# Layer 1's experts for 64 tokens by gathered rows, and GpSimd passes moved

## The chip, the core and the metric

The kernel runs on one core of a Trainium2 chip. Five engines work from queues of their own, in the order in which instructions were put there: TensorE (PE; its weight loads are PEld), VectorE (DVE), ScalarE (ACT), GpSimd (POOL) and SyncE (SP, which issues most DMAs). The metric is the device time of one execution, in microseconds.

## The reference, cut to what matters

Two layers act on 256 context and 256 latent tokens of width 1024. Layer 0 mixes by latent attention and retention, layer 1 by a gated delta net; after each mixer stands a norm and then PEER, a table of 16,384 experts:

```python
q = (xb @ w_q).reshape(PEER_BLOCK, PEER_HEADS, 2, half)
v1, i1 = lax.top_k(s1, PEER_TOPK)          # 16 best of 128 keys, twice
sc, j = lax.top_k(cand, PEER_TOPK)         # 16 best of the 256 sums, per head
gate = jax.nn.softmax(sc.astype(F32), axis=-1)
act = jax.nn.gelu(jnp.einsum('phkd,pd->phk', u_tab[e_idx], xb))
return jnp.einsum('phk,phkd->pd', gate * act, v_tab[e_idx])
```

So a token has 8 heads x 16 = 128 slots, each an expert with a row of 1024 in `u_tab` and one in `v_tab`. Layer 0 does this for all 512 tokens (four blocks of 128), layer 1 for the 256 latent ones (two blocks). Only the latent tokens are returned.

## The kernel before

**Two ways to compute PEER.** The dense way (`Dense`) runs over all 16,384 experts in 128 chunks of 128. Per chunk, `act` multiplies the chunk's u table (stationary, 128x128) by the tokens' columns (moving), 8 slices of depth; ScalarE takes gelu; VectorE multiplies by the tokens' weights for these experts, which `route` has spread into a table W in DRAM; and `products` multiplies the result (stationary, 128 experts x 128 tokens) by the chunk's v table (moving, two halves of 512 columns) into PSUM sums f that stay there over the whole stage. Two chunks form a group. The other way (`Rows`) takes 128 tokens as partitions and gathers for each of the 128 slots one row per token: GpSimd issues the indirect DMA, VectorE reduces u row times token to one value, and adds gate times v row to `rowy`. Before, layer 0 has three dense blocks (384 columns) and one by rows; layer 1 has two dense blocks (256 columns).

**Precision.** Every fp32 operand of the large products is split into a high part, rounded to the one-pass type fp32r, and a low part (`split`): ScalarE copies the high part (ush, vsh, gsh), VectorE or GpSimd subtracts (usl, vsl, gsl), and `mm3` makes three matmuls: high-high, high-low, low-high.

**Stages of one PEER.** `route` first chooses: per query table j a projection (pq), scores (sc), and scans for the 16 best on VectorE; the query tables' splits are GpSimd's (usl at L271), except the first two. Then it decodes gates and expert numbers and spreads them into W, 16 tokens at a time. Beside both, `Dense.early` computes the act values of the first chunks (36 and 24) and puts them to DRAM (gelud). Then `Dense.run` goes through the chunks; `fill` hangs other work on chunk numbers: in layer 0 the reductions for later modulation vectors (ada units, adaj at L341), the rows' steps, and `affine`, the first norm's scale and shift of four token tiles by GpSimd (L425, L426), and in layer 1 `affine` of two tiles at chunk 2.

**Who sets the order.** The loops only say what depends on what, and in which order of preference. The instructions of each engine are put in their order when the program is built, by a scheduler that takes what it holds to be ready; the queues then run in that fixed order. A step that hangs on a late chunk may stand much earlier in a queue.

**The first mixer.** 16 projections (z) and the retention values (rvp) with weight splits by GpSimd (arwl), beside 24 ada units on VectorE. `modulate` (L443 to L447) turns four slices of the normed tokens after another into hp: transposes, scale and shift on VectorE, high part by ScalarE, low part by VectorE and GpSimd in turn.

Of the kernel before, what the change touches and what calls it, by code (L numbers as in the profile page):

```python
# [47 lines left out]
RING = 4, 3  # L48
# [90 lines left out]
def layout(i):  # L139
# [42 lines left out]
    a["p_v"] = np.ascontiguousarray(i["peer_v"].reshape(2, NE, P, D))  # L182
    a["p_ur"] = np.ascontiguousarray(i["peer_u"][0])
# [59 lines left out]
class Model:  # L243
# [186 lines left out]
    def modulate(self, pool, ps, l, m, x, s, hs, i0, ln):  # L430
# [8 lines left out]
        for k in range(KD):  # L439
# [6 lines left out]
            nc.scalar.copy(hs[0][:, k, sl], t)  # L446
            (nc.gpsimd if k % 2 else nc.vector).tensor_sub(hs[1][:, k, sl], t, hs[0][:, k, sl].bitcast(F32))  # L447
# [20 lines left out]
    def mixer0(self, open_x, open_h):  # L468
# [150 lines left out]
        with ExitStack() as e2:  # L619
# [9 lines left out]
            weave(low(), pipe([key()] + [ret_proj(j) for j in range(4, 16)], 2), units())  # L629
            weave(ret_v())  # L630
# [143 lines left out]
        with ExitStack() as e2:  # L774
            p = self.pool(e2, "m0o", 1, side="right")
            w = []
            for k in range(KD):
                r = p.tile([P, D], F32, tag="woutr", name=f"woutr{k}", bufs=3)
                nc.sync.dma_start(r, a["ar_out"][:, k, :])
                w.append(self.split(p, r, [P, D], f"wout{k}", eng=nc.gpsimd if k % 3 == 2 else nc.vector))  # L780
                next(rest, None)
# [31 lines left out]
    def route(self, l, hs, parts, ps, first, dense, e2, rows=None):  # L813
        nc, a, c = self.nc, self.a, self.c
        nb = sum(len(tbs) for tbs in parts)
        spread_tbs = [tb for tbs in parts for tb in tbs if rows is None or tb != rows.tb]
        wd = self.dram.tile([len(spread_tbs) * P // WG, P, NE, WG], F32, name=f"W{l}")
# [13 lines left out]
        nc.sync.dma_start(kT, a["p_k"][l])  # L831

# [56 lines left out]
        def choose(part):  # L889
# [6 lines left out]
            while True:  # L896
                ends = [next(g, pr) is pr for g in (pr, tp)]
                if all(ends):
                    return
                if ends[0]:  # L900
                    n += 1
                    step(1 + n % 2)
                yield
# [63 lines left out]
        def slots(tb):  # L967
            t = f"{l}{tb}"
            g = gates[tb][0]
            tr = ps.tile([P, 512], F32, tag="ps", name="tr" + t)  # L970
            for n in range(2):
                nc.tensor.transpose(tr[:, n * P:(n + 1) * P], place(tb, n), c["ident"])
# [9 lines left out]
        def spread(tb, HA):  # L982
            t = f"{l}{tb}"
            for gi in range(P // OH):
# [29 lines left out]
        for part in range(len(parts)):  # L1014
            weave(choose(part))
        eq_.close()
        dense.by = None
        for part, tbs in enumerate(parts):
# [3 lines left out]
            for i, tb in enumerate(tbs):  # L1022
                if i + 1 < len(tbs):
                    slots(tbs[i + 1])
                elif rows is not None:
# [6 lines left out]

    class Rows:
        def __init__(self, m, tb, pool):
            self.m, self.tb = m, tb
            self.h = pool.tile([P, D], F32, name="rowh")
            self.e = pool.tile([P, P], U32, name="rowe")
            self.g = pool.tile([P, P], F32, name="rowg")
            self.y = pool.tile([P, D], F32, name="rowy")
            self.act = pool.tile([P, P], F32, name="rowa")  # L1040


        def choose(self, g, ii, hs, ps):
            nc, c = self.m.nc, self.m.c
            nc.vector.scalar_tensor_tensor(self.e, ii[0], float(NE), ii[1], ALU.mult, ALU.add)
            nc.vector.tensor_scalar_mul(self.g, g.rearrange("p h k -> p (h k)"), 1.0 / 1024)
            nc.gpsimd.memset(self.y, 0.0)
            ts = slice(self.tb * P, (self.tb + 1) * P)
            for h in range(2):
                o = ps.tile([P, 512], F32, tag="ps", name=f"rowt{h}")  # L1050
                for i in range(4):
                    for z in range(2):
                        self.m.mm(o[:, i * P:(i + 1) * P], hs[z][:, 4 * h + i, ts].bitcast(F32), c["ident"], z == 0, z == 1)
# [3 lines left out]
        def steps(self, pool):  # L1057
            m, nc = self.m, self.m.nc
            tabs = m.a["p_ur"], m.a["p_v"][0].rearrange("n p d -> (n p) d")
            rows = {}  # L1060

            def gather(z, s):
                if 0 <= s < P:
                    t = rows[z, s] = pool.tile([P, D], F32, tag="row" + "uv"[z], name=f"row{'uv'[z]}{s}", bufs=RING[z])
                    nc.gpsimd.indirect_dma_start(t, None, tabs[z], bass.IndirectOffsetOnAxis(ap=self.e[:, s:s + 1], axis=0))  # L1065

            for s in range(RING[0]):
                gather(0, s)
            for s in range(P + LAG):
                if s < P:  # L1070
# [4 lines left out]
                gather(0, s + RING[0])  # L1075
                gather(1, s - LAG + RING[1])
                if s % 4 == 1 and 5 <= s < P + 4:
# [3 lines left out]
                if v >= 0:  # L1081
                    nc.vector.scalar_tensor_tensor(self.y, rows.pop((1, v)), self.g[:, v:v + 1], self.y, ALU.mult, ALU.add)  # L1082
# [3 lines left out]
    class Dense:  # L1086
        G = 2

        def __init__(self, m, l, hs, nb, pool, done):
            self.m, self.l, self.hs, self.nb, self.p, self.done = m, l, hs, nb, pool, done  # L1090
# [3 lines left out]
        def early(self, es, ps):  # L1094
            m, N = self.m, self.nb * P
# [5 lines left out]
        def ahead(self, order, ps):  # L1101
            m, nc, l = self.m, self.m.nc, self.l
            us = self.table(order[0])
            for n, c in enumerate(order):
# [10 lines left out]
                else:  # L1115
                    g = self.pg.tile([P, self.nb * P], F32, tag="gelus", name=f"gelus{l}{c}", bufs=3)
                    nc.scalar.activation(g, o[:, :self.nb * P], AF.Gelu)
# [9 lines left out]
        def product(self, o, us, k):  # L1127
            N = self.nb * P
            self.m.mm3(o[:, :N], (us[0][:, k, :], us[1][:, k, :]), (self.hs[0][:, k, :N], self.hs[1][:, k, :N]), k == 0, k == KD - 1)

        def gelu(self, c, o):
            N = self.nb * P
# [15 lines left out]
        def run(self, wd, pool, psa, psv, fill, sums=None, ready=None):  # L1148
            m, nc, l, nb, G, done = self.m, self.m.nc, self.l, self.nb, self.G, self.done
            N = nb * P  # L1150
# [4 lines left out]
            def fetch(c):  # L1155
                late = c >= NE - 2
                vr = (self.p if late else pool).tile([P, D], F32, tag="ur" if late else "vr", name=f"vr{l}{c}", bufs=2)
                nc.sync.dma_start(vr, m.a["p_v"][l, c])
# [5 lines left out]
            def weighted(c, vr):  # L1164
# [8 lines left out]
                gs = m.split(pool, g, [P, N], "gs", bufs=GBUFS[l])  # L1173
                return gs, vs or m.split(pool, vr, [P, D], "vs", bufs=VBUFS[l])

# [628 lines left out]
```

## Time and profile before

| | |
|---|---|
| median of 3 runs | 3058.61 us (3046.81 to 3059.09) |
| profiled execution | 3056.68 us, span 3054.9 us, mean TensorE clock 0.955 |
| busy share of the span | PE 91%, PEld 79%, DVE 74%, ACT 42%, POOL 21% |
| DMA | 643.85 MB, 211 GB/s over the span |
| layer 0's dense stage | about 727 to 1692 us |
| layer 1's dense stage | about 2375 to 3037 us |

Matmul durations overlap each other, so TensorE's pace is read from starts, from the chain of waits or from counts in a window, and not from a mean duration. A window's row gives for each engine its busy time in the window and, in brackets, its instructions.

### The profile page before, as it was taken

To read this page: it belongs to the slowest core of one execution; us is meant where nothing else is said; L and a number is where in the kernel's file an instruction comes from. 1 tells how busy PE (TensorE), PEld (TensorE's weight loads), DVE (VectorE), ACT (ScalarE), POOL (GpSimd) and SP (SyncE) were. 2 spreads that over 40 slices of the span, in tenths; PEclk is the share of its full clock that TensorE was granted. 3 is DMA by queue.
4 is the path that set the end of the run, shared out by engine and by line. 5 is a ranking of instruction groups with operands and counts; after the bars stand their busy time and mean duration, and the time that the engine had idled before them with its cause. 6 is when DMAs were issued, how large, how long until landed. Compare 5 with 4: busy or idle time off the path is not lost.

```text
span 3054.9 us, 44722 instructions
## 1 busy us (share of the span) xinstructions
PE 2773.7 (91%) x16867; PEld 2412.5 (79%) x16867; DVE 2249.5 (74%) x4414; ACT 1291.4 (42%) x2176; POOL 643.4 (21%) x413
## 2 busy tenths in 40 slices
PE   7988898987999789999999899678878899999997
PEld 4766788986788688888899677667877689999996
DVE  2976599796999898999744578876898655555555
ACT  3335333674333233333333356333457454444443
POOL 2410134001036765666100000122400100000000
PEclk9999899998999999999999899788999999999999
DMA  6531223668999799999744123313348866666763
GB/s 231 186 121 45 95 89 109 232 236 318 325 360 390 284 400 374 394 397 395 250 153 135 57 73 94 91 56 119 117 152 296 262 221 207 215 213 207 214 206 110
DMA packets 272168, 643.85 MB, mean 211 GB/s; under 512 B 36464, under 2 KB 138992, under 8 KB 267472
## 3 DMA queue, kind: packets, MB, share of 16 engines
q1 hardware_dynamic: 225120, 487.50, 47.7%
q0 software_dynamic: 38768, 142.49, 12.0%
q10 hardware_dynamic: 8064, 11.01, 1.0%
q8 instruction: 132, 2.16, 0.3%
q14 instruction: 84, 0.69, 0.1%
HBM read 583.77 MB, written 57.15 MB: 210 GB/s over the span
## 4 chain that ended last, share of the span: by engine, by line
PE 35%; DVE 13%; issue 9%; DMA 8%; POOL 5%; ACT 3%; POOLq 0%; DVEq 0%; ACTq 0%; SPq 0%
PE f L254 14%; PE act L254 13%; DMA rowv<-p_v,rowe 3%; PE dz L254 3%; DMA vr<-p_v 2%; POOL rowv L1065 2%; POOL rowu L1065 2%; DMA ur<-p_u 1%; DVE usl L271 1%; DVE vsl L271 1%; DVE cv L1332 1%; DVE rowu L1072 1%; PE qb L254 1%; DVE adaj L341 1%; DVE rowy L1082 1%
## 5 line engine op out<-in xcount | busy, mean ns | idle before, releaser
L254 PE MATMUL f<-vsl,gsh 128*128 128x512 f32 x1260 | 498.2, 397 | 29.2 <-DVE vsl L271 29.1
L254 PE MATMUL f<-vsh,gsh 128*128 128x512 f32 x1260 | 488.8, 397 | 23.7 <-ACT vsh L268 11.9
L254 PE MATMUL f<-vsh,gsl 128*128 128x512 f32 x1260 | 494.2, 394 | 7.0 <-DVE gsl L271 7.0
L271 DVE TENSOR_TENSOR vsl<-vr,vsh 128x1024 fp32r<-128x1024 f32 x252 | 304.2, 1239 | 193.9 <-ACT vsh L268 193.4
L271 DVE TENSOR_TENSOR usl<-ur,ush 128x1024 fp32r<-128x1024 f32 x240 | 293.8, 1225 | 182.4 <-ACT ush L268 180.8
L268 ACT ACTIVATE ush<-ur 128x1024 fp32r<-128x1024 f32 x256 | 270.3, 1056 | 268.5 <-PE act L254 165.9
L254 PE MATMUL act<-hp0h,usl 128*128 128x384 f32 x1024 | 348.1, 340 | 19.2 <-DVE usl L271 12.4
L254 PE MATMUL act<-hp0h,ush 128*128 128x384 f32 x1024 | 349.1, 341 | 3.6 <-ACT ush L268 3.3
L254 PE MATMUL act<-hp0l,ush 128*128 128x384 f32 x1024 | 346.7, 339 | 0.0
L268 ACT ACTIVATE vsh<-vr 128x1024 fp32r<-128x1024 f32 x252 | 257.6, 1053 | 207.9 <-PE f L254 141.1
L268 ACT ACTIVATE gsh<-gelu 128x384 fp32r<-128x384 f32 (+1 forms) x256 | 120.4, 471 | 490.7 <-DVE gelu L1172 380.7
L254 PEld LDWEIGHTS f<-vsl,gsh 128*128 128x128 f32 x1260 | 240.1, 191 | 85.9 <-DVE vsl L271 39.5
L254 PEld LDWEIGHTS f<-vsh,gsh 128*128 128x128 f32 x1260 | 238.6, 191 | 81.7 <-ACT vsh L268 22.8
L254 PE MATMUL act<-hp1h,usl 128*128 128x256 f32 x1024 | 292.6, 286 | 8.3 <-DVE usl L271 8.3
L254 PE MATMUL act<-hp1h,ush 128*128 128x256 f32 x1024 | 293.2, 286 | 1.3 <-ACT ush L268 1.2
L254 PE MATMUL act<-hp1l,ush 128*128 128x256 f32 x1024 | 292.3, 285 | 0.0
L254 PEld LDWEIGHTS f<-vsh,gsl 128*128 128x128 f32 x1260 | 240.0, 190 | 58.1 <-DVE gsl L271 8.4
L1065 POOL DMA_INDIRECT rowu<-p_ur,rowe x128 | 173.9, 1358 | 272.6 <-DVE rowa L1072 180.1
L254 PEld LDWEIGHTS act<-hp0h,usl 128*128 128x128 f32 x1024 | 195.0, 190 | 21.5 <-DVE usl L271 13.7
L1065 POOL DMA_INDIRECT rowv<-p_v,rowe x128 | 190.8, 1490 | 100.0 <-DVE rowy L1082 77.3
L254 PEld LDWEIGHTS act<-hp1h,usl 128*128 128x128 f32 x1024 | 198.4, 194 | 9.4 <-DVE usl L271 9.2
L254 PEld LDWEIGHTS act<-hp1h,ush 128*128 128x128 f32 x1024 | 198.7, 194 | 3.8 <-ACT ush L268 1.7
(777 smaller groups left out, 5810.8 us busy)
## 6 DMA issues: line engine op xcount, KB each, us to landing
ur<-p_u SPq DMA_DIRECT2D x256, 512.0 KB
vr<-p_v SPq DMA_DIRECT2D x256, 512.0 KB
adat<-ada_t SPq DMA_DIRECT2D x80, 512.0 KB
W<-wst SPq DMA_DIRECT2D x20, 2048.0 KB
w<-W SPq DMA_DIRECT2D x32, 768.0 KB
wq<-p_wq SPq DMA_DIRECT2D x32, 512.0 KB
dw<-dn_in SPq DMA_DIRECT2D x32, 512.0 KB
w<-W SPq DMA_DIRECT2D x32, 512.0 KB
```

The costliest lines, as they stand in the source:

```text
L254: self.nc.tensor.matmul(out, l, r, start=start, stop=stop)
L268: nc.scalar.activation(hi, x, AF.Copy)
L271: (eng or nc.vector).tensor_sub(lo, x, hi.bitcast(F32))
L341: nc.vector.tensor_tensor_reduce(j, w, self.crow[:, s, :], op0=ALU.mult, op1=ALU.add, scale=1.0, scalar=self.c["ada_c"][:, l, m, k:k + 1], ...
L1065: nc.gpsimd.indirect_dma_start(t, None, tabs[z], bass.IndirectOffsetOnAxis(ap=self.e[:, s:s + 1], axis=0))
L1072: nc.vector.tensor_tensor_reduce(u, u, self.h, op0=ALU.mult, op1=ALU.add, scale=1.0, scalar=0.0, accum_out=self.act[:, s:s + 1])
L1082: nc.vector.scalar_tensor_tensor(self.y, rows.pop((1, v)), self.g[:, v:v + 1], self.y, ALU.mult, ALU.add)
L1332: (nc.gpsimd if CONV[j] == "p" else nc.vector).scalar_tensor_tensor(co, xp[:, :ns, q:q + T], cw[:, j, q:q + 1], co, ALU.mult, ALU.add)
```

## The change

- Layer 1: the second block's last 64 tokens go by rows, the other 192 densely. Two slots go at a time: partitions 0 to 63 hold the 64 tokens' slots 0 to 63, partitions 64 to 127 the same tokens' slots 64 to 127, so that 64 gathers of u rows and 64 of v rows do. For even v rows ScalarE scales a folded identity by the gates and TensorE adds two products (fp32) into a PSUM bank `yr`; odd ones go to `rowy` on VectorE.
- Dense with 192 columns: act has 192 moving columns. The half block's high and low parts stand side by side as one 128-column stationary tile, so its product takes two matmuls and not three; the two parts are added at the end (`ys`).
- The first norm's scale and shift leave the dense stages (`affine`) for the choice stage (`scaled`), still on GpSimd.
- First mixer: weight splits on VectorE; 8 of the 24 ada units go beside the retention values; output splits on VectorE.
- `modulate`: high part straight from PSUM by ScalarE, all low parts on VectorE.
- Layer 1's gate rows and second norm's rows go from the stage's start to its middle; layer 0's ada units end at 0.87 of the stage instead of 0.97; its rows are spaced over four chunks more.

```diff
-            nc.scalar.copy(hs[0][:, k, sl], t)
-            (nc.gpsimd if k % 2 else nc.vector).tensor_sub(hs[1][:, k, sl], t, hs[0][:, k, sl].bitcast(F32))
+            nc.scalar.activation(hs[0][:, k, sl], o[:, :T], AF.Identity, bias=sh[:, k:k + 1], scale=sc[:, k:k + 1])
+            nc.vector.tensor_sub(hs[1][:, k, sl], t, hs[0][:, k, sl].bitcast(F32))
...
-            return self.split(pw, w, shape, "arw", eng=nc.gpsimd)
+            return self.split(pw, w, shape, "arw")
...
-            weave(low(), pipe([key()] + [ret_proj(j) for j in range(4, 16)], 2), units())
-            weave(ret_v())
+            sums = units()
+            weave(low(), pipe([key()] + [ret_proj(j) for j in range(4, 16)], 2), islice(sums, 2 * KD))
+            weave(ret_v(), until=sums, steps=3)
...
+        def scaled():
+            gb = p.tile([P, 2, D], F32, tag="A", name=f"lgb{l}")
+            for i, z in enumerate("gb"):
+                nc.gpsimd.dma_start(gb[:, i, :], a[f"ln1_{z}"][l])
+            for t in x:
+                nc.gpsimd.tensor_mul(t, t, gb[:, 0, :])
+                yield
+                nc.gpsimd.tensor_add(t, t, gb[:, 1, :])
+                yield
...
+                if n % 4 == 0:
+                    next(scale, None)
...
-            for gi in range(P // OH):
+            for gi in range(min(P, dense.N - tb * P) // OH):
...
+        def halves(self, acc, w, t, first, last):
+            for h in range(2):
+                self.m.mm(acc[h * 64:h * 64 + 64, :], w, t[:, h * 512:(h + 1) * 512], first, last)
...
+                    if acc is not None and v % 2 == 0:
+                        d = pool.tile([P, n], F32, tag="rowd", name=f"rowd{l}{v}", bufs=3)
+                        nc.scalar.activation(d, self.fold, AF.Copy, scale=self.g[:, v:v + 1])
+                        self.halves(acc, d, t, v == 0, False)
+                    else:
+                        nc.vector.scalar_tensor_tensor(self.y, t, self.g[:, v:v + 1], self.y, ALU.mult, ALU.add)
...
+                        if half:
+                            for z in range(2):
+                                m.mm(acc[tb][h], gs[:, whole:whole + P], vs[z][:, hl], first and z == 0, last and z == 1)
...
-        def affine():
-            rows = m.norm_rows(pa, 0, 1, "adat")
-            for t in x[:4]:
-                m.affine(nc.gpsimd, t, rows)
...
+            rows = m.Rows(m, 1, 1, True, m.pool(ed, "rows1", 1, side="right"))
+            dense = m.Dense(m, 1, h, P + HALF, *pools1, EARLY[1])
...
+            fill, at = {}, paces(EARLY[1], 24, 20)
+            fill[at(0.5)] = [prepare]
+            for i in range(rows.n + LAG):
+                fill.setdefault(at(0.12 + 0.88 * i / (rows.n + LAG)), []).append(lambda: next(steps))
+            last = dense.run(wd, *pools, fill)
```

**The order, GpSimd, layer 0's choice stage.** Before, after the output splits (wout5l): low halves of the modulations (hp0l), the memset of `rowy`, then the splits of query tables (usl):

```order
L447 TENSOR_TENSOR hp0l<-hf_2500,hp0h 128x256
L1047 MEMSET rowy 128x1024
L447 TENSOR_TENSOR hp0l<-hf_2599,hp0h 128x256
L447 TENSOR_TENSOR hp0l<-hf_2613,hp0h 128x256
L447 TENSOR_TENSOR hp0l<-hf_2627,hp0h 128x256
L447 TENSOR_TENSOR hp0l<-hf_2641,hp0h 128x256
L271 TENSOR_TENSOR usl_2781<-wq_2778,ush_2780 128x1024
L271 TENSOR_TENSOR usl_2833<-wq_2830,ush_2832 128x1024
```

Now, at the same place; x are token tiles, lgb the norm's rows:

```order
L1070 MEMSET rowy_2658 128x1024
L839 DMA lgb_2869<-ln_g 128x1024
L839 DMA lgb_2869<-ln_b 128x1024
L841 TENSOR_TENSOR x<-x,lgb_2869 128x1024 x2
L843 TENSOR_TENSOR x<-x,lgb_2869 128x1024 x2
L841 TENSOR_TENSOR x<-x,lgb_2869 128x1024 x2
L272 TENSOR_TENSOR usl_2781<-wq_2778,ush_2780 128x1024
L843 TENSOR_TENSOR x<-x,lgb_2869 128x1024 x2
L272 TENSOR_TENSOR usl_2833<-wq_2830,ush_2832 128x1024
```

Six passes and two loads stand ahead of the first query split, two more ahead of the second; the low halves are gone from this queue.

**The order, VectorE, start of layer 1's dense stage.** Before, after the last spread product (A at L996), tables' low parts (usl, vsl) and the weighted gelus:

```order
L996 TENSOR_TENSOR A_21486<-O_21487,iT_20457 128x1408
L271 TENSOR_TENSOR usl_21551<-ur_21548,ush_21550 128x1024
L271 TENSOR_TENSOR usl_21584<-ur_21581,ush_21583 128x1024
L271 TENSOR_TENSOR usl_21617<-ur_21614,ush_21616 128x1024
L271 TENSOR_TENSOR usl_22301<-ur_22298,ush_22300 128x1024
L271 TENSOR_TENSOR usl_22334<-ur_22331,ush_22333 128x1024
L271 TENSOR_TENSOR vsl_21718<-vr_21706,vsh_21717 128x1024
L271 TENSOR_TENSOR vsl_21727<-vr_21708,vsh_21726 128x1024
L1172 TENSOR_TENSOR gelu_21572<-gelu_21572,w_21710 128x256
```

Now, from the last usl before the first vsl on; ISA with rowu is the reduction of a gathered u row:

```order
L272 TENSOR_TENSOR usl_21311<-ur_21308,ush_21310 128x1024
L1117 ISA rowu_22099,rowa_18850<-rowu_22099,rowh_18846 128x1024
L1117 ISA rowa_18850 128x1
L272 TENSOR_TENSOR vsl_21428<-vr_21416,vsh_21427 128x1024
L1117 ISA rowu_22101,rowa_18850<-rowu_22101,rowh_18846 128x1024
L1117 ISA rowa_18850 128x1
L272 TENSOR_TENSOR vsl_21437<-vr_21418,vsh_21436 128x1024
L1117 ISA rowu_22103,rowa_18850<-rowu_22103,rowh_18846 128x1024
L1117 ISA rowa_18850 128x1
L1117 ISA rowu_22105,rowa_18850<-rowu_22105,rowh_18846 128x1024
```

Reductions stand before and between the first v splits; of the 64, 18 come in the first six chunks and all before the 37th vsl.

**The order, GpSimd, layer 1's dense stage.** Before, this queue holds four row loads and the affine there. Now, near the end of the u gathers (rowu) and the start of the long run of v gathers (rowv):

```order
L1110 DMA rowu_26838<-p_ur,rowe_18847 128x1024
L1110 DMA rowu_26922<-p_ur,rowe_18847 128x1024
L1110 DMA rowu_27040<-p_ur,rowe_18847 128x1024
L1110 DMA rowv_22921<-p_vr,rowe_18847 128x1024
L1110 DMA rowv_22964<-p_vr,rowe_18847 128x1024
L1110 DMA rowv_23080<-p_vr,rowe_18847 128x1024
```

Five v gathers stand among the u gathers, the other 59 behind the last of them.

## Rows read from the trace of the kernel before

**Rows 1.** Chain of waits, layer 1's dense stage: start us, us, what.

```profile
2499.21 5.47 PE f L254 x24
2504.67 5.75 PE act L254 x48
...
3021.09 13.64 PE f L254 x60
```

**Rows 2.** Windows, layer 1's dense stage: PE, PEld, DVE, ACT, POOL, PEclk, DMA share, GB/s.

```profile
2375.00:2516.00 141.00, 128.70 (x656) 106.44 (x656) 87.52 (x118) 65.42 (x95) 6.37 (x3) 0.97 0.74 236
2516.00:3037.00 521.00, 521.00 (x3335) 476.08 (x3334) 294.35 (x377) 246.06 (x367) 0.00 (x0) 1.00 0.65 201
...
2420.00:2440.00 20.00, 17.52 (x79) 12.98 (x78) 13.72 (x20) 10.48 (x15) 0.00 (x0) 1.00 0.97 319
```

**Rows 3.** Windows, layer 0's dense stage while rows are gathered.

```profile
950.00:1000.00 50.00, 49.08 (x247) 44.02 (x246) 47.04 (x64) 15.81 (x24) 31.35 (x22) 1.00 1.04 395
1000.00:1050.00 50.00, 41.52 (x201) 37.57 (x200) 43.80 (x54) 14.50 (x21) 31.80 (x22) 0.90 0.90 323
1050.00:1100.00 50.00, 36.78 (x176) 32.88 (x175) 40.10 (x46) 11.87 (x18) 37.07 (x23) 0.90 0.78 297
...
1300.00:1350.00 50.00, 50.00 (x255) 45.48 (x254) 47.42 (x66) 16.70 (x26) 31.63 (x23) 1.00 1.04 401
```

**Rows 4.** Windows, layer 0's choice of experts, and layer 1's spread.

```profile
400.00:420.00 20.00, 20.00 (x101) 16.96 (x100) 19.83 (x128) 6.06 (x9) 7.19 (x3) 1.00 0.28 96
...
2300.00:2320.00 20.00, 17.66 (x192) 16.47 (x190) 20.00 (x20) 16.66 (x41) 0.00 (x0) 0.91 0.73 268
```

**Rows 5.** Windows, first mixer's projections.

```profile
100.00:125.00 25.00, 25.00 (x111) 20.64 (x110) 24.72 (x30) 5.02 (x7) 12.66 (x5) 1.00 0.52 172
...
150.00:175.00 25.00, 20.14 (x79) 15.41 (x79) 24.46 (x43) 7.70 (x10) 9.51 (x4) 0.93 0.60 200
```

**Rows 6.** Tiles adaj, V: count, duration ns min/median/max, first and last start.

```profile
L341 DVE CUSTOM_DVE_ANT_0 adaj<-adat,c_row,small x48: 1268/1283/3466, 69.2 to 173.1; 128x1024 f16<-128x1024 f32 x48
...
L835 DVE MAX8 V<-S x96: 274/286/306, 384.1 to 2232.3; 128x8 f32<-128x128 f32 x96
...
L883 DVE TENSOR_TENSOR cand<-V x64: 164/200/2419, 394.7 to 2234.3; 128x32 f32<-128x32 f32 x24, 128x64 f32<-128x64 f32 x16, 128x96 f32<-128x96 f32 x8, 128x48 f32<-128x48 f32 x8
```

**Rows 7.** Tiles abp, tr, or: weight loads (PEld) and matmuls.

```profile
L254 PEld LDWEIGHTS abp<-hp0h,abh x8: 108/108/170, 1736.7 to 1748.2; 128*32 128x32 f32 x8
...
L254 PEld LDWEIGHTS tr<-R,XA x16: 192/192/192, 2090.9 to 2092.6; 128*128 128x128 f32 x16
L254 PE MATMUL tr<-R,XA x16: 275/275/275, 2091.0 to 2092.7; 128*128 128x128 f32 x16
...
L254 PE MATMUL or<-sd,rv x96: 379/379/431, 204.6 to 256.5; 128*64 128x256 f32 x96
```

**Rows 8.** Timeline, TensorE: start us, us, what; weights before moving operand.

```profile
217.28 2.81 PE L254 MATMUL or<-sd,rv 128*64 128x256 f32 x24
...
2091.04 1.95 PE L254 MATMUL tr<-R,XA 128*128 128x128 f32 x16
```

**Rows 9.** Groups by line and shape: spread on VectorE, splits on GpSimd.

```profile
L994 DVE TENSOR_TENSOR O<-iT,c_iota 128x2048 f16<-128x2048 f16 x80 | 95.7, 1236 | 0.0
L995 DVE TENSOR_TENSOR A<-O,iT 128x2048 f16<-128x2048 f16 x40 | 49.4, 1236 | 0.0
L996 DVE TENSOR_TENSOR A<-O,iT 128x1408 f16<-128x1408 f16 x40 | 36.1, 903 | 0.0
...
L271 POOL TENSOR_TENSOR arwl<-arw,arwh 128x1024 fp32r<-128x1024 f32 x16 | 43.2, 2699 | 92.9 <-ACT arwh L268 85.6 <-PE z L254 7.3
```

**Rows 10.** Timelines: GpSimd in layer 0's dense stage, VectorE at layer 1's start.

```profile
1049.86 13.13 POOL L426 TENSOR_TENSOR x<-x,lb 128x1024 f32<-128x1024 f32 x4 [5.12 <-DMA lb<-ln_b]
...
2373.76 5.41 DVE L1172 TENSOR_TENSOR gelu<-gelu,w 128x256 f32<-128x256 f32 x3 [2.88 <-DMA w<-W]
```

More of the change, by code (lines that the diff above doesn't have):

```diff
@@ L47 @@
 AHEAD = 1
-RING = 4, 3
+RING = (4, 3), (4, 3)
 LAG = 8
@@ L970, in slots @@
             tr = ps.tile([P, 512], F32, tag="ps", name="tr" + t)
+            ii = [place(tb, n) for n in range(2)]
             for n in range(2):
-                nc.tensor.transpose(tr[:, n * P:(n + 1) * P], place(tb, n), c["ident"])
+                nc.tensor.transpose(tr[:, n * P:(n + 1) * P], ii[n], c["ident"])
+            if rows is not None and rows.tb == tb:
+                rows.choose(g, ii, hs, ps)
             nc.tensor.transpose(tr[:, 2 * P:3 * P], g.rearrange("p h k -> p (h k)"), c["ident"])
@@ L1680, in pair, with paces @@
             return [pool.tile([P, KD, n], F32R, name=nm + z) for z in "hl"]
+        def paces(done, first, second):
+            cost = np.cumsum([second if c < done else first + second for c in range(NE - 2)])
+            return lambda share: int(np.searchsorted(cost, min(share, 1.0) * cost[-1]))
         def phase(name):
@@ L1771, in build @@
             psv = m.pool(ed, "psv1", 1, PSUM)
             pools = (m.pool(e2, "densew1", 1), m.pool(e2, "psa1", 2, PSUM), psv)
+            yr = psv.tile([P, 512], F32, tag="yr", name="yr")
+            steps = rows.steps(m.pool(ed, "rowring1", 1, side="right"), yr)
             pn = m.pool(ed, "ln1", 1, side="right")
-            rows = m.norm_rows(pn, 1, 2)
-            gates = m.gates(pn, psm, 1, 2, (1,))
-            def affine():
-                rows = m.norm_rows(pn, 1, 1)
-                for t in x[2:4]:
-                    m.affine(nc.gpsimd, t, rows)
@@ L1782, in build, with prepare @@
-            last = dense.run(wd, *pools, {2: [affine]})
+            lns, gates = [], {}
+            def prepare():
+                lns.extend(m.norm_rows(pn, 1, 2))
+                gates.update(m.gates(pn, psm, 1, 2, (1,)))
+            fill, at = {}, paces(EARLY[1], 24, 20)
[3 more added lines that the diff above has]
+            last = dense.run(wd, *pools, fill)
@@ L1783, in build, with ys @@
+            def ys(tb):
+                o = last(tb)
+                if tb == 0:
+                    return o
+                for h in range(2):
+                    y = rows.h[:, h * 512:(h + 1) * 512]
+                    nc.scalar.copy(y[:HALF], o[h][HALF:])
+                    nc.vector.tensor_add(y[:HALF], y[:HALF], o[h][:HALF])
+                    nc.scalar.copy(y[HALF:], yr[h * HALF:(h + 1) * HALF])
+                return [rows.h[:, h * 512:(h + 1) * 512] for h in range(2)]
             for tb in range(2):
-                m.norm(pn, x[2 + tb], last(tb), gates[1])
+                m.norm(pn, x[2 + tb], ys(tb), gates[1])
```

179 lines of the change are left out of this document (96 added, 83 removed).

## The prediction

> **What bounds the kernel now.** I read the chain of waits first, from its end backwards, then the windows by stage, then the rows of single tiles. The chain shows layer 1's dense stage as a strict alternation on TensorE, 48 act matmuls in 5.75 us and 24 f matmuls in 5.47 us, with nothing in between, until the last 60 f [rows 1]. So one group (two chunks) costs 11.22 us: 0.1198 us an act matmul (256 columns) and 0.2279 us an f matmul (512 columns). The windows split the stage [rows 2]: 521 us of this alternation (46.4 groups), in which TensorE is never idle, and a front of 141 us for the first 36 chunks, most of whose act values were made earlier. In the 521 us VectorE is 56% busy and DMA moves 201 GB/s: there is room beside TensorE, and only what shortens TensorE's own work pays.
>
> Layer 0's dense stage is another matter. While its rows are gathered, DMA stands at 401 GB/s with a share of 1.04 and VectorE at 47 of 50 us [rows 3]: gathers, tables and vector work bound it together with TensorE. In the choice of experts VectorE is full (19.83 of 20 us), and in the spread of layer 1 too (20.00 of 20) [rows 4]. The first mixer has TensorE and VectorE full at once, and loses a little TensorE time near its end [rows 5].
>
> **What a GpSimd pass does to VectorE.** Three rows of tiles settle what "GpSimd out of" is worth [rows 6]. An ada reduction takes 1.28 us, at worst 3.47; the small sums of candidates 0.20, at worst 2.42; the scans for maxima 0.286, never above 0.306. The first two read two SBUF tiles and are held up by about 2 us when a GpSimd pass over 128x1024 is under way; the scans read one and are not.
>
> **The change, part by part.**
>
> *Layer 1, the 521 us.* f has 20 matmuls a group instead of 24, since the half block takes two and not three: 20 x 0.2279 = 4.56 us. Act matmuls have 192 columns instead of 256. No row shows such a matmul at this type. At the price of columns it would be 192/2.4 + 13 ns of what 256 columns leave over, 0.0935 us; with no gain at all 0.1198. But each one also brings a new 128-column weight tile. The load of 32 columns takes 108 ns and that of 128 takes 192, so 0.875 ns a column and 112 ns for 128, and the narrowest stream with a new 128-column load each time runs at (1.95 - 0.275)/15 = 0.1117 us [rows 7, 8]. That row is the nearest and I take 0.1117: 48 x 0.1117 = 5.36 us. For every second slot two half-width fp32 matmuls of 512 columns are added. The row of 64-column pairs with 256 columns gives (2.81 - 0.379)/23 = 0.106 us each [rows 7, 8], so about 0.21 each at 512, 0.42 a pair, and 33 pairs over 46.4 groups make 0.30 us a group (twice that if the halves don't overlap). Sum 10.22 against 11.22 us: -46 us. Each pair also adds a wait in TensorE's queue, for a gathered row and for ScalarE's scaled fold, with act and f behind it. At 2.2 MB a group plus 0.7 MB of rows, DMA needs 285 GB/s where 401 has been had [rows 3], so I give these waits 4 us. VectorE's load grows from 6.3 us a group (294.35/46.4) by about 1 us. Term: **-42 us**.
>
> By the Trainium skill ("TensorE: Matmul & The Clock Gate", LDWEIGHTS) a weight load costs its columns divided by 1.2, 107 ns for 128, however narrow the moving side is; that speaks against going below 256 columns. Taken as the price of an act matmul, the term would be 10 us larger; the trace has 112 per load and 111.7 per matmul, and I keep the row.
>
> *Layer 1, the front.* The order puts all 64 u gathers and their reductions before the 37th v split; the v gathers follow, most of them after the last u. So the front has to move 64 x 0.52 = 33.5 MB of rows beside 18.9 MB of v tables, 5 of u tables, 5.5 of weights and stored gelus: 63 MB, 158 us at 401 GB/s, and I add 7 us for a start in which VectorE waits for the first gathers with the v splits behind them. TensorE needs 360 x 0.2279 + 10 x 24 x 0.1117 = 109 us there, so DMA becomes the bound. 165 for 141 us: **+24 us**. The lower end is no loss (the gathers find idle DMA: 236 GB/s now [rows 2]), the upper end the 319 GB/s that the front has reached with smaller transfers: 204 us, +63.
>
> *Layer 1, spread.* 12 groups of 16 tokens instead of 16, VectorE-bound: 4 x (2 x 1.236 + 1.236 + 0.903) = -18 us [rows 9]. Added are ten small vector operations, 32 matmuls of 0.11 and some copies to build indices, gates and the folded rows: +4. **-14 us.**
>
> *The affine of the first norm, moved.* In layer 0 eight GpSimd passes ran in the dense stage; four took 13.13 us in one piece [rows 10], no gather was issued meanwhile, and the two windows around them have 201 and 176 matmuls where 247 stood before [rows 3]: (494 - 377)/247 x 50 = 24 us, and I take 22. They now stand in the choice stage with their two loads of 512 KB, on GpSimd's queue ahead of the splits of the third and fourth query table, with TensorE's projections behind those. Six passes of 2.5 us in front of the third split make it some 5 us late, and the low halves of the second modulation, now on VectorE and reading two tiles, are held up too; the scans that fill this stage are not [rows 6]. +8, so **-14 us** (0 to -22). In layer 1 four passes held the first gelu products (three took 5.41 us [rows 10]), while the stage also waited for its weights; -7 there, +4 in the choice: **-3 us.**
>
> *First mixer.* 20 splits of 2.7 us [rows 9] leave GpSimd. VectorE gets 20 x 1.23 = 25 us and is spared up to 20 x 2 us of hold-ups, and 8 of 24 ada units move behind the projections, over the last 96 matmuls. TensorE was at 79 matmuls in 25 us (0.228 x 79 = 18) in 150 to 175 us [rows 5]: at most 7 us to win there, and a few more before. **-5 us** (+4 to -12). If VectorE's queue, with ada units ahead of the splits, is later than GpSimd was, the sign turns.
>
> *The rest.* Low halves of modulations on VectorE cost 0.4 us a slice and save a trip to GpSimd; output splits likewise; the gate rows in mid-stage are 8 short matmuls that were idle time before and now are not, 1 us; the new sum at the end, copies and additions with nothing beside them, 3 us. Ada units and rows in layer 0 are spaced differently, but the order still finishes its rows at the same chunk: 0. **+2 us.**
>
> Sum: -42 + 24 - 14 - 14 - 3 - 5 + 2 = -52. The profiled execution took 3056.7 us (span 3054.9), 1.9 below the median 3058.6: 3004.7, and 3006.6 beside the median. Prediction 3006 us.
>
> **Rivals.**
> 1. *The load hides behind a narrow matmul.* For it: the loads' time need not add to the spacing of 256 columns. Against: 0.1117 at half the columns. Price: (0.1117 - 0.0935) x 48 x 46.4 = 41 us more saved: 2965. The Trainium skill (same page, Back-to-back issue gap) gives about 81 ns for a sustained load and matmul of 128 columns, which would put 192 columns at the columns' price; no run here shows it at this type. 0.16.
> 2. *The front is worse.* Gathers and table loads share DMA worse than in layer 0, since VectorE takes a row before each early split and only four u rows are in flight: +39 to the forecast's front, 3045; a band of 3030 to 3070. 0.17 (0.04 faster, 0.08 same, 0.05 slower).
> 3. *The other side: below 256 columns this type runs in two passes, as fp32 does.* fp32 streams 128 columns in 0.1117 us, two cycles a column [rows 8], and all rows of the one-pass type have 256 or more. Then an act matmul costs 2 x 192/2.4 + 5 = 165 ns, 0.053 x 48 x 46.4 = 119 us more: 3125. It decides from 0.135 us on, where 52 us are eaten. 0.08, slower.
> 4. *The moved passes only move their loss* (layer 0's -14 and the mixer's -5 become 0): 3025. 0.09 (0.07 faster, 0.02 same).
>
> **How the numbers follow.** The forecast has 0.50: 2985 to 3040, of it 0.48 faster and 0.02 same (an act matmul without any gain, +18, is inside). A difference under 0.5%, 15 us, can't be told from none here. Faster: 0.48 + 0.16 + 0.04 + 0.07 = 0.75. Same: 0.02 + 0.08 + 0.02 = 0.12. Slower: 0.05 + 0.08 = 0.13. The range leaves out rival 3, the upper edge of 2 and the lower edge of 1: 2958 to 3068.
>
> **What would show it.** Right: in the chain, 48 act matmuls in 5.4 us and 20 f in 4.6; the last third of the span at about 10.2 us a group; all u reductions within about 165 us of the dense stage's start at DMA near 400 GB/s; no dip in layer 0's dense stage around its middle; spread shorter by 15 us or so. Wrong: 48 act in 4.5 (rival 1) or 7.9 us (rival 3); a front above 190 us (rival 2); a projection in layer 0's choice that waits for GpSimd by more than 15 us (rival 4).

## The result and the profile after

The changed kernel takes 3084.18 us (median of 7 runs, 3073.93 to 3088.12) against 3058.61: ratio 1.0084, 95% interval 1.0063 to 1.0105. It is 0.8% slower, where 3006 us, 1.7% less than before, was forecast. The profiled span went from 3054.9 to 3084.6 us, 29.7 more.

The act and f matmuls of layer 1 came out as predicted; here is the chain of waits in the last third (start us, us, what), against [rows 1]:

```profile
2600.28 4.78 PE f L255 x20
2605.06 5.34 PE act L255 x48
2611.40 4.78 PE f L255 x20
2616.18 5.34 PE act L255 x48
2621.51 4.57 PE f L255 x20
```

48 act take 5.34 us (0.1113 each; forecast 0.1117), 20 f 4.57. But 5.34 us after 2605.06 is 2610.40, and the next f starts 1 us later. TensorE's timeline shows what stands there:

```profile
2610.32 1.08 PE L255 MATMUL yr<-rowv,rowd 128*64 128x512 f32 x4
2611.33 0.50 PE L255 MATMUL f<-vsh,gs 128*128 128x512 f32 x1
```

The windows, against [rows 2, 3 and 5] (columns as there): layer 0's dense stage, the first mixer, then layer 1's front and its later stage.

```profile
1000.00:1050.00 50.00, 47.84 (x242) 42.87 (x242) 46.53 (x64) 17.10 (x26) 30.11 (x23) 1.00 1.03 402
1050.00:1100.00 50.00, 49.55 (x251) 44.56 (x249) 47.96 (x66) 19.46 (x29) 31.83 (x22) 1.00 1.03 401
...
150.00:175.00 25.00, 23.91 (x106) 19.48 (x104) 16.61 (x35) 5.38 (x8) 0.54 (x1) 1.00 0.36 113
...
2360.00:2530.00 170.00, 116.79 (x473) 91.54 (x473) 130.66 (x253) 49.27 (x89) 78.83 (x62) 0.79 0.95 338
...
2600.00:2700.00 100.00, 100.00 (x653) 86.45 (x652) 67.11 (x103) 49.76 (x84) 21.64 (x14) 1.00 0.82 293
```

The dip in layer 0 is gone (493 matmuls where 377 were) and the mixer holds TensorE busy to its end. The loss is in the front: TensorE is busy 117 of 170 us, and there at a mean granted clock of 0.79, while DMA's share is 0.95 and VectorE works 131 us. The waits of that front (2362 to 2540; us in total, times, longest) show who stands before whom. Gathers wait for buffers that VectorE frees. ScalarE waits for v tables, and for VectorE's sums before the gelu of each four row sums (rowa). TensorE waits for ScalarE: for its splits (vsh, gs) and for its gelu of act sums.

```profile
POOL rowu L1110 <- DVE rowa L1117: 64.2, 24, 8.5
ACT vsh L269 <- DMA vr<-p_vr: 55.0, 20, 6.7
ACT rowa L1119 <- DVE rowa L1117: 40.6, 9, 9.9
DVE rowu L1117 <- DMA rowu<-p_ur,rowe: 21.3, 15, 3.1
...
PE f L255 <- ACT gs L1233: 17.7, 4, 7.5
PE f L255 <- ACT vsh L269: 17.0, 9, 5.0
...
PE act L255 <- ACT gelu L1190: 15.0, 4, 5.4
```

To place each microsecond I compare when the same matmul starts in both profiles (f by sixteenths of its count in a layer; 128 chunks, so a quarter is 32). Before, layer 0's f last until 1713 us, past the 1692 given above.

| stretch | before us | after us | difference | forecast |
|---|---|---|---|---|
| start to the last retention value (rvp) | 187.2 | 173.9 | -13.3 | -5 |
| attention, to the last oa | 114.7 | 119.6 | +4.9 | 0 |
| second modulation, to the first pq | 66.4 | 72.4 | +6.0 | +8, with the choice |
| choice and spread, to layer 0's first f | 359.0 | 357.5 | -1.5 | |
| layer 0's f, first to last | 986.2 | 973.3 | -12.9 | -22 |
| to layer 1's first pq | 446.8 | 453.7 | +6.9 | +4, with the next |
| choice, to layer 1's first act | 60.7 | 62.5 | +1.8 | |
| spread, to the last wp | 131.0 | 117.9 | -13.1 | -14 |
| to the first f, and a quarter of f | 158.3 | 226.3 | +68.0 | +24 - 7 |
| the rest of f | 527.1 | 506.9 | -20.2 | -42 |
| end | 17.5 | 20.6 | +3.1 | +3 |

The differences make 29.7. Two rows hold nearly all of the miss: the front, 51 us worse than forecast, and the rest of f, 22 worse. These are single profiles: in the 13 of this document whose layer 0 has the changed kernel's code, layer 0's f take 966.2 to 975.5 us, so a few us there say nothing.

### The profile page after: what moved, and what is told of

Same layout as the page of the kernel before. It is cut to its first block, busy times and chain, and to the rows that moved or that the text cites. A ratio compares the mean times of both kernels' runs of the same rounds, so it can differ in the third digit from the quotient of the medians.

```text
span 3084.6 us, 44894 instructions
## 1 busy us (share of the span) xinstructions
PE 2758.7 (89%) x16679; PEld 2366.2 (77%) x16679; DVE 2328.5 (75%) x4753; ACT 1273.8 (41%) x2195; POOL 743.8 (24%) x500
## 4 chain that ended last, share of the span: by engine, by line
PE 35%; DVE 15%; DMA 12%; issue 8%; POOL 3%; ACT 3%; POOLq 0%; DVEq 0%; ACTq 0%; SPq 0%
PE act L255 13%; PE f L255 13%; DMA vr<-p_vr 6%; PE dz L255 3%; DMA rowv<-p_vr,rowe 3%; POOL rowu L1110 2%; DVE vsl L272 2%; POOL rowv L1110 2%; DMA ur<-p_u 1%; DMA rowu<-p_ur,rowe 1%; DVE usl L272 1%; PE yr L255 1%; DVE rowu L1117 1%; DVE rowy L1133 1%; DVE adaj L342 1%
## 5 line engine op out<-in xcount | busy, mean ns | idle before, releaser
L255 PE MATMUL f<-vsh,gs 128*128 128x512 f32 x2268 | 760.3, 404 | 60.3 <-ACT vsh L269 26.9
L255 PEld LDWEIGHTS f<-vsh,gs 128*128 128x128 f32 x2268 | 437.5, 194 | 176.3 <-ACT vsh L269 37.5
L255 PE MATMUL f<-vsl,gs 128*128 128x512 f32 x1260 | 505.9, 403 | 25.6 <-DVE vsl L272 23.6
L1110 POOL DMA_INDIRECT rowv<-p_vr,rowe x192 | 276.9, 1442 | 497.8 <-DVE rowy L1133 312.5
L255 PEld LDWEIGHTS f<-vsl,gs 128*128 128x128 f32 x1260 | 244.7, 194 | 87.7 <-DVE vsl L272 37.5
L255 PE MATMUL act<-hp1h,ush 128*128 128x192 f32 x1024 | 292.1, 285 | 21.5 <-ACT gelu L1190 15.0
L255 PE MATMUL act<-hp1h,usl 128*128 128x192 f32 x1024 | 291.2, 284 | 21.8 <-DVE usl L272 21.8
L255 PE MATMUL act<-hp1l,ush 128*128 128x192 f32 x1024 | 289.8, 283 | 0.0
L1117 DVE CUSTOM_DVE_ANT_0 rowu<-rowu,rowh 128x1024 f32<-128x1024 f32 x192 | 232.9, 1219 | 31.9 <-DMA rowu<-p_ur,rowe 31.7
L255 PEld LDWEIGHTS act<-hp1l,ush 128*128 128x128 f32 x1024 | 205.9, 201 | 2.4
```

Of the source, the lines that this page charges most:

```text
L255: self.nc.tensor.matmul(out, l, r, start=start, stop=stop)
L1117: nc.vector.tensor_tensor_reduce(u, u, self.h, op0=ALU.mult, op1=ALU.add, scale=1.0, scalar=0.0, accum_out=self.act[:, s:s + 1])
```

## The experiments

Periods of a group are means over the sixth to the fifteenth sixteenth of layer 1's f (40 groups), "front" is its first quarter; both from single profiles. A time without a ratio is that of a single run, except where the text says otherwise.

**Layer 1 undone alone.** `Dense(m, 1, h, P + HALF, ...)` becomes `Dense(m, 1, h, T, ...)`, and rows, their steps and `yr` go.

> Layer 1 goes back to 256 dense tokens without rows; everything else of the change stays (affine in the choice stage, VectorE's splits, layer 0's spacing, gate rows in mid-stage). Theory 1 (layer 1's rows lose, the rest gains): the dense stage of layer 1 is as before, 662 us from the first to the last f matmul, 11.22 us a group; the rest keeps its 12 us lead at the start of layer 1's spread: 3045 to 3050 us, faster than before by about 0.3 to 0.45%. Rival (the edits outside of layer 1 lose, the rows only look guilty): 3058 or more.

3023.48 us, ratio to before 0.9887 (0.9864 to 0.9910): beyond the expected gain, and 60 us below the changed kernel. Groups take 11.22 us again, and the front 129 us:

```profile
2349.00:2478.00 129.00, 122.78 (x633) 101.67 (x632) 78.45 (x112) 62.68 (x91) 0.00 (x0) 0.99 0.78 246
```

The loss belongs to layer 1's rows, and the rest of the change gains 35 us: of the profile's 32.6, 18.9 lie in layer 0's f and 14.5 in layer 1's spread and front (from its first act to a quarter of its f 274.8 us instead of 289.3), where affine passes and gate rows no longer stand (which of the two gives how much was not tried). From layer 1's first act to the end the two profiles differ by 52.7 us: rows save 8.5 of spread and 20.3 of f, and cost 78 up to the end of the front and 3.6 at the end. Another 9.6 us between these two profiles lie ahead of that act, 6.0 of them in layer 0's f, where both have the same code; they are not the rows' doing as far as this shows.

**What fills the front: gathers or sums.** First all gathers, with reductions over 64 of 1024 columns:

```diff
-  nc.vector.tensor_tensor_reduce(u, u, self.h, ...
+  k = 64 if self.half else D
+  nc.vector.tensor_tensor_reduce(u[:, :k], u[:, :k], self.h[:, :k], ...
```

> The changed kernel with all u rows of layer 1 still gathered, but each reduction reads only 64 of its 1024 columns (the rest of the sums is left out). Theory A (the front is bound by DMA: 33 MB of rows beside the tables): the first quarter of layer 1's f still takes 175 to 196 us, DMA share 0.9 or more. Theory B (VectorE's queue is what delays it: 64 x 1.22 us of reductions with waits, splits of v behind them): 125 to 150 us.

3078.2 us, front 186 us. Then all reductions, with only the first four u rows gathered (`rows[z, s] = self.four[s % ring[0]]`):

> The changed kernel with all 64 full reductions of layer 1, but only the first four u rows are gathered (the others sum over these four again, so layer 1's row part is left out). Theory A (DMA bounds the front): the first quarter of layer 1's f takes 125 to 150 us. Theory B (VectorE's queue): 170 to 196 us, with DMA below 300 GB/s.

3055.1 us, front 165 us. The window 2360 to 2530 of the one and of the other:

```profile
2360.00:2530.00 170.00, 119.16 (x490) 94.16 (x490) 80.50 (x263) 53.73 (x96) 64.78 (x62) 0.77 0.95 344
```
```profile
2360.00:2530.00 170.00, 130.27 (x623) 104.95 (x623) 149.93 (x288) 65.85 (x114) 3.42 (x2) 0.85 0.59 190
```

Each alone lengthens the 129 us: gathers by 57, sums by 36, both by 66. With gathers DMA's share is 0.95, with sums VectorE is nearly full (150 of 170 us). Theory A holds for the first run and is wrong for the second (125 to 150 expected); B is wrong for the first and 5 us too high for the second. There are two bounds, one behind the other, the gathers' the longer. What TensorE's lower clock adds in the front is not separated.

By the waits, the sums reach TensorE less through the v splits than through ScalarE, which itself stands before VectorE's results. Waits of the run with sums, in the same window, then ScalarE's and TensorE's timelines around the longest of TensorE's:

```profile
ACT rowa L1123 <- DVE rowa L1121: 31.9, 10, 7.0
...
PE f L255 <- ACT gs L1237: 13.6, 3, 5.9
PE act L255 <- ACT gelu L1194: 12.6, 3, 7.1
...
PE f L255 <- DVE vsl L272: 5.7, 12, 0.7
```
```profile
2503.91 0.20 ACT L1123 ACTIVATE rowa<-rowa 128x4 f32<-128x4 f32 x1 [4.63 <-DVE rowa L1121]
...
2504.97 0.31 ACT L1194 ACTIVATE gelu<-act 128x192 f32<-128x192 f32 x1
```
```profile
2505.33 0.53 PE L255 MATMUL act<-hp1h,ush 128*128 128x192 f32 x1 [7.11 <-ACT gelu L1194]
```

ScalarE stands 4.63 us before the gelu of four row sums that VectorE has not finished. A split and the gelu that TensorE needs stand behind it, and TensorE is idle for 7.11 us. No run takes this gelu out of ScalarE's queue, so its share of the 36 us stays open.

**More buffers.** `RING` of layer 1 from (4, 3) to (6, 3).

> The changed kernel with six buffers of u rows in layer 1 instead of four; the order is the same. Theory A (the front reached 336 GB/s instead of 400 because too few transfers were under way: gathers wait for a buffer that VectorE frees): DMA at 370 to 400 GB/s there, the first quarter of layer 1's f 165 to 180 us instead of 196, total 3055 to 3070. Theory B (336 GB/s is what this mix of transfers gives at a share of 0.95): 190 to 196 us and 3080 to 3088.

3078.38 us, ratio to before 1.0063 (1.0042 to 1.0084); front 186.5 us, 344 GB/s in 2360 to 2530 at the same share of 0.95. Between the two, nearer to theory B: at a share of 0.95 this mix gives 338 to 344 GB/s, with four buffers or six and also with the sums cut short; the 400 of layer 0 came at a share of 1.04 [rows 3]. What keeps the share at 0.95 is not shown.

**The pair's price.** Streams of 64 instead of 512 columns in `halves`.

> The changed kernel, with the half-width fp32 matmuls of the even v rows streaming 64 columns instead of 512 (so 448 of 512 columns of these sums are left out), all gathers, waits and weight loads as they were. Theory 1 (a pair costs what its four instructions stream, 4 x 0.21 us and some filling): a group with a pair takes 10.2 to 10.4 us instead of 11.0, 32 x 0.7 = 20 to 24 us saved, 3060 to 3065. Rival (a pair costs its wait, for the gathered row or for ScalarE's scaled fold): nothing saved, 3080 to 3088.

3058.24 us (median of 10 runs), 26 us less, and the group falls from 10.84 to 10.33; the front of this profile is 5 us shorter too, so the total lies 2 us beyond the 3060 expected. The tile yr in the changed kernel, and in this one (instructions, ns min/median/max):

```profile
L255 PE MATMUL yr<-rowv,rowd x128: 592/618/643, 2567.1 to 3033.1; 128*64 128x512 f32 x128
```
```profile
L255 PE MATMUL yr<-rowv,rowd x84: 221/246/271, 2601.7 to 2892.1; 128*64 128x64 f32 x84
```

From the first of four to the next f it takes 1.01 us there and 0.26 here: the theory holds, the pair is streaming, not waiting.

**Is 0.1113 the load or the columns?** `N = P if self.l else self.N` in `product`.

> The changed kernel with layer 1's act matmuls at 128 columns instead of 192 (the gelu of the half block then stands on sums of other tokens, so its part of layer 1 is left out), each still with a new 128-column weight tile. If the spacing of 0.1113 us at 192 columns is the weight load, it stays 0.111 and 48 act take 5.34 us again; if it is the columns, it falls to 0.067 to 0.085 us and 48 take 3.2 to 4.1 us.

The chain of waits of this kernel:

```profile
2703.38 5.31 PE act L255 x48
2708.69 1.01 PE yr L255 x4
2709.70 4.76 PE f L255 x20
```

48 act in 5.31 us: a third fewer columns change nothing (3076.6 us in one run, inside the range of the changed kernel). So columns do not set the spacing between 128 and 192. That the load of 128 weight columns does fits the 112 ns a load worked out from [rows 7], and the run above, where four instructions with 64 weight columns each take 0.26 us together; but no run changed the weights' columns at this type.

**Rows spread over the stage.** First attempt: the gather's indices are copied by an instruction that also reads the newest gelu tile.

```diff
+  nc.vector.scalar_tensor_tensor(q, m.now[:, :4].bitcast(F32), 0.0, self.ef[:, s:s + 4], ALU.mult, ALU.add)
```

> The changed kernel, with each four gathers' indices copied by VectorE from a step that also reads the newest gelu tile (times zero), so that no gather can be issued before the chunk that the code names; rows then begin at chunk 28 and run to the end. Theory 1 (the front is long because 33 MB of u rows crowd into it): the first quarter of layer 1's f takes 115 to 135 us instead of 196; the groups after it carry the u rows and take 10.8 to 11.2 us, VectorE at about 90% and DMA near 350 GB/s there; total 3010 to 3040. Rival (the front is long for another reason: late indices, late weights, TensorE's lower clock): first quarter 180 us or more, 3075 to 3090. Second rival (the rows cost the same wherever they stand, since VectorE's or DMA's time is what counts): front short, but groups of 12 us, 3070 to 3090.

3153.99 us, ratio 1.0299 (1.0269 to 1.0328). The front fell to 158 us, not to 115 to 135, and groups rose to 13.55 us: worse than either rival. Waits of the window 2600 to 2900 (us in total, times, longest):

```profile
ACT rowa L1132 <- DVE rowa L1130: 92.1, 8, 13.2
...
PE act L255 <- ACT gelu L1203: 49.4, 8, 8.4
DVE rowu L1130 <- DMA rowu<-p_ur,rowq: 49.3, 22, 6.0
...
DVE rowy L1146 <- DMA rowv<-p_vr,rowq: 27.0, 7, 5.8
```

VectorE stands before rows that were asked for too late, with gelu products and splits behind them in its queue. ScalarE stands eight times before the gelu of four row sums, and all that TensorE waits (49.4 of 300 us) are eight waits for a gelu of ScalarE's. With all v rows on VectorE as well (`if False:` for the even ones):

> As the paced kernel, and in addition all 64 v rows are summed on VectorE, none on TensorE (only the last folding of the two halves stays there). Theory 1: the 32 pairs cost TensorE about 1.1 us each, so the groups fall towards 9.91 us (48 x 0.1113 + 20 x 0.2279), while VectorE then has 9.2 to 10 us of work a group: groups of 9.9 to 10.6 us, 2985 to 3025. Rival (VectorE with its queue in order becomes the bound): groups above 10.8 us, slower than the paced kernel, 3040 or more.

3166.86 us, ratio 1.0356 (1.0324 to 1.0388), groups 13.43 us: the rival holds. TensorE's pairs are gone and nothing is won, since TensorE waits (239 of 300 us busy, 251 in the run before).

Second attempt: the sum is held back, not the gather.

```diff
+  nc.vector.tensor_scalar_mul(self.act[:, s:s + 1], m.now[:, :1].bitcast(F32), 0.0)
```

> The changed kernel, with each u row's reduction held back (by a one-column write that reads the newest gelu tile), while its gather may go as soon as a buffer is free: the rows run from chunk 28 to the end, and each gather has four reductions' time to land. Theory (the first pacing lost because VectorE, in order, stood 3 to 6 us before each group of four reductions for rows just asked for): front 120 to 130 us, groups of 10.8 to 11.6 us, total 2990 to 3040. Rival (VectorE's queue, 85 to 90% full in order with waits for rows in it, is what starves TensorE): groups of 12 us or more, 3080 to 3160.

3121.79 us, ratio 1.0218 (1.0205 to 1.0232): front 136 us, groups 13.16, the rival's number. Yet VectorE is busy only 192 of 300 us; it waits for v rows now:

```profile
POOL rowu L1110 <- DVE rowa L1119: 86.7, 21, 7.1
DVE rowy L1135 <- DMA rowv<-p_vr,rowe: 81.5, 16, 8.0
```

Five buffers of v rows (`RING` (4, 5)):

> The second paced kernel (3122 us) with five buffers of v rows instead of three, so that each v gather may be issued two slots earlier. Theory (late v rows in VectorE's queue, 104 us of waits in 400, starve TensorE; VectorE's own work, 65%, does not): those waits fall below half, groups go from 13.2 to 11 to 12 us, 3030 to 3080. Rival (the gathers' common queue on GpSimd, in order behind waits for u buffers, sets it): little changes, 3105 to 3125.

3113.0 us, groups 12.82: VectorE's waits for v rows fell from 81.5 to 57.7 us, not below half, and the time by 9 (1 us under the fastest of the runs before), as the rival has it. So again each half alone, with the second pacing:

> The second paced kernel (3122 us) with all its reductions, but only the first four u rows gathered (the others sum over these four again, so layer 1's row part is left out). Theory (gathers that land late in ordered queues starve TensorE): groups fall from 13.2 to 10.8 to 11.3 us, 2985 to 3020. Rival (the sums on VectorE, 1.3 us each in front of splits, do it): groups stay above 12.3 us, 3080 or more.

> The second paced kernel with all its gathers, but each u reduction reads 64 of 1024 columns (the rest of the sums is left out). Theory (late gathers): groups stay above 12.3 us, 3080 or more. Rival (the sums): 10.8 to 11.5 us, 2990 to 3030.

Sums without u gathers: 3028.2 us, groups 10.95 (the group as the theory has it, the time 8 us above). Gathers without sums: 3090.0 us, groups 12.61, as the theory has it. The same 300 us of the one and of the other, and in each VectorE's wait for v rows:

```profile
2600.00:2900.00 300.00, 297.70 (x1955) 256.99 (x1955) 237.12 (x417) 145.22 (x249) 58.98 (x40) 0.99 0.80 279
```
```profile
DVE rowy L1139 <- DMA rowv<-p_vr,rowe: 24.9, 9, 6.0
```
```profile
2600.00:2900.00 300.00, 265.79 (x1610) 225.57 (x1609) 172.77 (x359) 123.79 (x212) 101.08 (x67) 0.93 0.81 291
```
```profile
DVE rowy L1136 <- DMA rowv<-p_vr,rowe: 90.0, 16, 7.8
```

VectorE may be 79% busy with sums and TensorE still runs through; at 58% with gathers it starves. What starves is not VectorE's time or DMA's share (0.80 and 0.81) but the landing of rows for which an ordered queue waits. Which queue is decisive, GpSimd's (a v gather behind one that waits for a u buffer), VectorE's, or ScalarE's as in the first attempt, stays open.

**The moved passes.** On top of layer 1 undone, the affine passes wait for the last gathered row (layer 0) and for mid-stage (layer 1), by a one-column write to their weights' tile.

> As the kernel with 256 dense tokens in layer 1 (3023 us), but the affine passes of the first norm leave the choice stage: in layer 0 they wait for the last gathered row and run in the last third of the dense stage, where VectorE is 40% busy and no gather is issued, in layer 1 they wait for the middle of its dense stage. Theory (the moved passes hold up the second modulation's low halves, three of which took 6.3 us where three took 1.15 without a pass beside them): the first projection of layer 0's choice starts 6 us earlier, that of layer 1 3 us earlier, nothing is lost in the dense stages: 3012 to 3017. Rival (a GpSimd pass costs its price wherever it stands, also in the last third of the dense stage): 3020 to 3030.

3018.17 us, ratio 0.9876 (0.9861 to 0.9892), the fastest of all, between theory and rival; the interval overlaps that of 3023, so only the profiles tell them apart. The low halves in the second modulation on VectorE's timeline, in the changed kernel without a GpSimd pass beside them (at 341 us) and with one (at 358 us), and here:

```profile
341.10 1.15 DVE L448 TENSOR_TENSOR hp0l<-hf,hp0h 128x256 fp32r<-128x256 f32 x3
...
358.53 6.30 DVE L448 TENSOR_TENSOR hp0l<-hf,hp0h 128x256 fp32r<-128x256 f32 x3
```
```profile
353.71 1.14 DVE L448 TENSOR_TENSOR hp0l<-hf,hp0h 128x256 fp32r<-128x256 f32 x3
```

The first pq starts at 356.0 instead of 366.2 us (some of it from attention), layer 1's way from the last f of layer 0 to its first act is 6.5 us shorter; but layer 0's f take 8.8 us longer than in the kernel of 3023 us (976.1 us; the 13 profiles named above have 966.2 to 975.5). GpSimd's timeline here, the window of that stretch, and the same window in the kernel of 3023 us:

```profile
1471.29 6.11 POOL L426 TENSOR_TENSOR x<-x,lateg 128x1024 f32<-128x1024 f32 x2 [2.88 <-DMA lateg<-ln_g]
...
1489.40 6.05 POOL L427 TENSOR_TENSOR x<-x,lateb 128x1024 f32<-128x1024 f32 x2
```
```profile
1450.00:1500.00 50.00, 49.08 (x233) 44.11 (x234) 42.58 (x32) 15.65 (x23) 30.12 (x13) 0.93 0.56 195
```
```profile
1450.00:1500.00 50.00, 48.72 (x247) 44.03 (x247) 30.21 (x33) 17.35 (x24) 4.84 (x3) 1.00 0.63 207
```

About as many VectorE instructions (32 and 33) take 42.6 us beside the passes and 30.2 without, and TensorE makes 233 matmuls instead of 247, by estimate some 3 us at the 5 matmuls a us of that kernel: the rival is right for so much. The rest of the 8.8 us is not clear of the spread between profiles.

**The mixer's splits back.** `self.split(pw, w, shape, "arw", eng=nc.gpsimd)` in the kernel of 3018.

> The kernel of 3018 us (256 dense tokens in layer 1, late affine passes) with the 20 low halves of the first mixer's weights back on GpSimd. Theory (these splits held up VectorE by their lock, as the two-input sums of 3.47 us showed, and came late themselves): the last projection of the first mixer ends 6 to 13 us later than at 175 us, of which attention gives back up to 5: 3023 to 3030. Rival (the gain before the attention came from the moved ada sums alone): 3015 to 3021.

3030.13 us, ratio 0.9915 (0.9894 to 0.9936). The theory holds, at the upper edge of its range: the last rvp ends at 190.4 instead of 175.4 us, 15 later and beyond the 6 to 13 expected. The row of the ada sums in the changed kernel, and here:

```profile
L342 DVE CUSTOM_DVE_ANT_0 adaj<-adat,c_row,small x128: 1266/1278/1314, 69.9 to 1379.0; 128x1024 f16<-128x1024 f32 x128
```
```profile
L342 DVE CUSTOM_DVE_ANT_0 adaj<-adat,c_row,small x128: 1268/1278/3422, 70.0 to 1386.7; 128x1024 f16<-128x1024 f32 x128
```

The hold-ups (longest 1.31 us without, 3.42 us with) come and go with GpSimd's splits.

## Why the prediction was wrong, step by step

- **Layer 1's front (+24) failed first.** Measured were +68 in the table, where the moved passes (forecast -7) are in it and the first f comes 30.6 us after the last wp instead of 22.7; against the kernel with layer 1 undone the rows cost 78. The prediction bounded the term at +63. The order was read rightly: all 64 u sums stand there, and the last ended at 2533.7 us, 172 us after the first f (165 forecast). What failed is the overlap: the f of 36 chunks were to fit into DMA's time, and by then only 28 were done; 36 took 217 us. Two assumptions fell. DMA was priced at layer 0's 401 GB/s. The bytes were right (196 us at 321 GB/s make 62.9 MB, 63 forecast), but DMA gave 338 at a share of 0.95, and 344 with more buffers. And VectorE got no price at all beyond 7 us of start: 64 sums of 1.22 us stand in front of v splits in its own queue, and ScalarE's queue waits for their results; they cost 36 us even without gathers. Rival 2, given 0.17, names this mechanism; its price of 39 above the forecast's front was too low too, and of its two reasons the four rows in flight are worth only 9 us (front with six buffers).
- **Layer 1's other 521 us (-42) had one term wrong.** Act (5.36 us forecast, 5.34 measured) and f (4.56, 4.57) were right to 0.02 us. The pair was priced as two instructions of 0.21 us. The program has two products, but the trace shows 132 instructions for 66 products, 0.25 us each in the mean (the two of a product start within 0.01 us, the next product 0.47 us later): 1.01 us a pair, 1.2 with the change-over to f (4.78 instead of 4.57 us). The `or` rows from which 0.106 us was taken count instructions too (96 for the 48 products in the code), so the factor of two could have been seen. 32 pairs make 38 us instead of the 18 counted with their waits, and -42 became -20. The waits that I feared were small.
- **Rivals 1 and 3** fell with 0.1113 us: neither 0.0935 (0.093 by its own sum) nor 0.165. The Trainium skill ("TensorE: Matmul & The Clock Gate", LDWEIGHTS) puts a weight load at its columns divided by 1.2, by estimate 107 ns for 128. The trace's spacing agrees to about 4%, with 0.1106 us at 128 moving columns and 0.1113 at 192; the load's own duration in [rows 7], 192 ns, does not. Rival 3 also misread its row: it took the 0.1117 us of [rows 8] for two cycles a column, where the forecast takes the same row for a load's price, and the `or` rows, 0.106 us for 256 columns, have one.
- **Spread (-14): -13.1**, right in the sum and in part by luck. Against the kernel with layer 1 undone the rows give 8.5 of it, and the other edits the rest, which had been priced at nothing here. In single profiles the spread takes 116 to 125 us with rows and 126 to 130 in the kernels with 256 dense tokens.
- **Affine, layer 0 (-14).** The dip of [rows 3] gave back 23.9 us in its sixteenth of the f (22 forecast), and the choice lost 6.0 us, by held-up low halves as named. But the other sixteenths lost 11 us, most of them in the fourth and the thirteenth. Ada units and rows spaced otherwise had been priced at nothing; that they do it, and which of the two, was not tried. Rival 4 was right for a quarter of the loss (6.0 of 23.9 us).
- **First mixer (-5): -13.3**, of which attention gave back 4.9. The window of [rows 5] showed 7 us of idle TensorE, and I took that for the limit; the way back cost 15. **Affine and gate rows, layer 1 (-3)**: 14.5 us in its spread and front, by the kernel with layer 1 undone; the front's lost time was there, larger than the 5.4 us piece of [rows 10]. On the way to layer 1's first act 8.7 us were lost where 4 were forecast; the kernel with late passes gives 6.5 back.
- **The rest (+2):** +3.1 at the end, 3 forecast; its other parts were not measured by themselves.
- **A reading without weight:** the front of 141 us before holds the f of 34 chunks (408), not of 36.

The error in the whole was to price the gathered rows by single resources. DMA, VectorE and the order of the queues each looked free by a third, as averages, and the order put all u rows where two of them were not.

## What to carry to other kernels

Price a hoisted block of gathers where the built order puts it, on every queue that it crosses: bytes at the rate of that stretch, and each sum in front of the work that TensorE waits for, also where another engine's queue stands behind its result. Count instructions, not products, for fp32 on TensorE. And where a GpSimd pass over SBUF is moved, look for the two-input VectorE work at its new place: here it paid 1.7 us an instruction (low halves, 6.30 us for three instead of 1.15) to 2.2 us (ada sums, [rows 6]).

## What the hardware showed that I had not expected

With a new 128-column weight tile each time, the one-pass matmul has a floor of 0.111 us at 128 and at 192 columns (0.1198 at 256): cutting columns from 256 to 192 won 7%, not 25%. And TensorE lost more to late gathers with VectorE's queue 58% busy (groups of 12.61 us) than to plain sums with it 79% busy (10.95 us).
